# Walking two chunk loops in step: matmuls of RWKV and gated delta issued in pairs

## The chip, the core and the metric

The kernel runs on one core of a Trainium2 chip. A core has TensorE (PE in the profile; its weight loads are shown apart as PEld), VectorE (DVE), ScalarE (ACT), GpSimd (POOL) and SyncE (SP), which issues most DMAs. The engines run side by side, each through its own queue in order, and wait for one another by semaphores. SBUF is the working memory; matmuls write to PSUM, which has eight banks. The metric is the device time of one execution in microseconds (us).

## The reference

One layer of a hybrid encoder over 512 tokens of width 2048:

```python
y = xn @ w_in[l]
o_gdn = _gdn_group(...)      # gated delta: 8 heads of 128
o_rwkv = _rwkv_group(...)    # RWKV-7: 16 heads of 64
h = h + jnp.concatenate([o_gdn, o_rwkv], axis=-1) @ w_out[l]
h = h + _cross_attention(...)             # 4 heads, 256 memory tokens
h = h + jnp.square(jax.nn.relu(hn @ mlp_w_up[l])) @ mlp_w_down[l]
return _rmsnorm(h, norm_final)
```

Both groups carry a state along the sequence. Gated delta is written in the reference over chunks: with products that are known ahead (`W`, `U`, `Aqk`, the decayed keys), a step of its scan is

```python
v_new = U_c - W_c @ S
o = qd @ S + A_c @ v_new
S = S * exp(gl) + kt.T @ v_new
```

RWKV is written token by token (`S = S * w_t + (S a_t) b_t^T + v_t k_t^T`, `o = S r_t`), and the kernel computes it in chunks as well. Everything is in float32; the large products are done in the kernel as three products of parts in fp32r (high times high, low times high, high times low), the small ones in f32.

## The kernel before

The kernel has a mixer part (input projections, gated delta, RWKV, the key side of the attention's projections), then the rest of the attention with the output projection, then the MLP. The change is in the mixer.

**The filler.** `projections` computes the 59 columns of the input projection, called py in the profile: a column is 128 outputs by 512 tokens, 48 matmuls of 128x128 weights by 512 tokens in fp32r. `evict` multiplies a finished column by the norm's factor on DVE and puts it in one of four buffers (`NY = 4`, tile y), from which the mixer reads it. Two PSUM banks (mm) take turns, so the matmuls of a column wait for the eviction of the column two before. After the columns come the key projections kp (also in `projections`), and then kq, which waits for the event that the last inverse of gated delta is done (`after("inverted", 7)`). py, kp and kq need weights that `loader` splits into a high and a low part on ACT and DVE.

**The two chains.** The mixer goes in eight rounds. Round j takes seven columns: three for `rwkv(j)` (r, k, v of two heads, 128 channels) and four for `gdn(j)` (k, q, v, z of one head). Each function is a chain of operations on all engines:

- `rwkv(j)`: decay and keys (`pW`, `pA`, `pn`, then the event front); the Gram products of the 8 chunks for both heads (tiles pgA and pgB, in two halves of four chunks; 64 rows deep, 128 columns), masked into GA and GB by DVE; the 16x16 blocks' inverse on POOL by way of DRAM (`inverse_blocks`); transposes and products with 64x64 matmuls (pk, pat, pv, pak, pkv); the inverse's upper levels (ri); `pu` and `pwt`; the chunk loop over 8 chunks (tile rs); and the outputs (po, pp). `rwkv(j+1)` begins before the chunk loop of j, but its Gram products wait until po of j is done.
- `gdn(h)`: convolutions of the columns, norms (gn), products (pkk, pqk), transposes (pkt, pvt), its own blocks' inverse on POOL and the upper levels (gi), the chunk loop over 4 chunks (tile gs), the outputs (gpo, gon). `gdn(h+1)` begins when `gdn(h)` has ended.

A step of RWKV's chunk loop has two matmuls, WTz by the state and BTz by U, of 128 rows and 64 columns (14 in all); one of gated delta has three, of 128 rows and 128 columns (10 in all). Between two matmuls of a loop stands one DVE operation, which reads the PSUM result and makes the next operand. RWKV's loop uses the one bank scr, gated delta's the one bank scg. The POOL inverse of the two chains shares a lock (`solving`): the second may begin, its load of the blocks included, only when the first is through.

**The order of the work.** All of it is issued by a planner that runs while the kernel is built. Each chain is a generator that yields one operation, a list of operations to be issued together, or a condition. `run` keeps a model clock for each engine, asks each chain for its next operation, and takes the one whose modelled start is first:

```python
key = (t + (0 if c[3][0][0] == "PE" else 150 * rank), rank)
```

The rank decides between equal PE starts, and for other engines it adds 150 ns a step: evictions have rank 0, the loader 2, rwkv and gdn 3, the projections 4. So a matmul of a chain goes before a py matmul that could start at the same time, and py takes all the rest. `cost` prices an operation and `start` gives its earliest time from the modelled ends of its inputs. The prices move the model's clocks and with them the order in which the operations of each engine are issued; the chip then runs each engine's queue in this order.

`cost` charges an fp32r matmul 0.417 ns a column and 13.3 ns after another of its kind, 120 ns after any f32 matmul; an f32 matmul is charged 100 ns more where the shape of its weights differs from that before and is not 128x128.

Of the kernel before, what the change touches and what calls it, by code (L numbers as in the profile page):

```python
# [10 lines left out]
F32R = mybir.dt.float32r  # L11
# [62 lines left out]
def build(tc, I, out):  # L74
# [132 lines left out]
    SL, SM = Lane(nc.sync, "SP", wait=6000.0), Lane(nc.sync, "SP", margin=8000.0)  # L207
    DV, AC, GS, TE, SY = (Lane(e, k) for e, k in ((V, "DVE"), (S, "ACT"), (GP, "POOL"), (PE, "PE"), (nc.sync, "SP")))

    def cost(op):  # L210
        eng, nm, _, a, k, out, ins, _ = op
        n = out.free_size()
        if eng == "PE":
            l = ins[0]
            if l.dtype == F32R:
                return n * 0.417 + (13.3 if state["shape"] is None else 120.0)
            sh = (l.partition_size(), l.free_size())
            sw = 0 if state["shape"] == sh or sh == (128, 128) else 100
            if nm == "transpose":
                return sw + (110 if sh[0] > 64 else 40)  # L220
            if sh == (64, 64):
                return sw + (32 if op[5].tensor.name[:2] in ("ri", "gi", "pa", "pv", "pu", "pw", "pk", "po", "pp") else 59)
            if sh[0] < 128 and n == 512:
                return sw + 530
            return sw + (115 if sh[0] < 128 and n == 128 else 2 * max(n * 0.84, 114))
        if eng == "DVE":
            if nm == "memset":
                return 60 + 0.3 * n
            if nm == "tensor_scalar":
                return 210 + 0.45 * n  # L230
# [21 lines left out]
    def issue(op):  # L252
        eng, nm, f, a, k, out, ins, slack = op
        t = start(op)
        d = cost(op)
        f(*a, **k)  # L256
        if nm == "dma_start":
            clock[eng] = t + (60 if eng == "ACT" else 620 if any(x.tensor.name[:2] in ("bg", "nd") for x in [out] + ins) else 330)
            size = math.prod(out.shape) * 4
            state["dma"] = max(state["dma"], t + 330) + size / 300  # L260
            t, eng = max(state["dma"] + 700, t + 2900) + slack[1], "DMA"
        else:
            t += d
            clock[eng] = t
        if eng == "PE":
            state["shape"] = None if ins[0].dtype == F32R else (ins[0].partition_size(), ins[0].free_size())
        if eng == "ACT" and len(a) > 2 and a[2] in (AF.Tanh, AF.Ln, AF.Exp):
            state["table"] = "l" if a[2] == AF.Ln else "e"
        landed[where(out)] = (t, eng)
        for i in ins:  # L270
            b = where(i)
            if seen.get(b, (0.0, 0))[0] < t:
                seen[b] = (t, eng)
# [7 lines left out]
    def after(*ev):  # L281
        return lambda: ev in events
# [282 lines left out]
    def projections():  # L565
# [4 lines left out]
        for n in range(2, NIN):  # L570
            if n == NSQ[3] + 3:
                yield after("macc")
                pt = psb("pms", "mm", 2)
                mc = ybuf[macc[0]]
                yield TE.matmul(pt[:, 0:M], ones, mc[:, 0:M], start=True, stop=False)
                yield TE.matmul(pt[:, 0:M], ones, mc[:, M:2 * M], start=False, stop=True)
                chain(memnorm(pt, mc[:, M:2 * M]), 1)
            if n >= 4:
                yield after("py", n - 2)
            pt = psb(f"py{n}", "mm", 2)  # L580
            yield from gemm_([pt], xhi, xlo, 2 * n, left="x" if n == NIN - 1 else None)
            chain(evict(n, pt), 0)
# [264 lines left out]
        yield DV.tensor_copy(big[hA, :, 64:128], v(A[:, 256:512])[hA])  # L847


    def rwkv(j):  # L850
        base = 3 + 7 * j
        js = slice(j * P, (j + 1) * P)
# [54 lines left out]
        G = [tl(f"G{nm}", shape=[P, 8, P]) for nm in "AB"]  # L907
        GA, GB = G
        for q in range(2):
            pgs = [psb(f"pg{nm}{j}_{q}") for nm in "AB"]  # L910
            for c in range(4):
                for pg, h in zip(pgs[::-1], (hB, hA)):
                    yield TE.matmul(pg[:, c * P:(c + 1) * P], flat(BK[h, q * 4 + c]), flat(AR[h, q * 4 + c]),
                                    start=True, stop=True)
            for pg, g in zip(pgs, G):
                yield DV.tensor_tensor(out=g[:, q * 4:q * 4 + 4, :], in0=pg.rearrange("p (c t) -> p c t", t=P),
                                       in1=K("mA").unsqueeze(1).broadcast_to([P, 4, P]), op=ALU.mult)
# [102 lines left out]
        if j < 7:  # L1020
# [6 lines left out]
        yield DV.tensor_tensor(out=lgs[64:96, P:2 * P], in0=lg[64:96, P:2 * P], in1=lgs[64:96, P:2 * P].bitcast(F32),  # L1027
                               op=ALU.subtract)

        for c in range(7):  # L1030
            if c > 0:
                p1 = psb(f"rs1_{j}_{c}", "scr", 1)
                yield TE.matmul(p1[:, 0:64], WTz[:, c - 1, :], Qs[:, CS[c]], start=True, stop=True)
                yield DV.tensor_tensor(out=U[:, CS[c]], in0=p1[:, 0:64], in1=U[:, CS[c]], op=ALU.add)
            p3 = psb(f"rs3_{j}_{c}", "scr", 1)
            lm, nx = lam[:, c:c + 1], CS[c + 1]
            if c > 0:
                yield DV.scalar_tensor_tensor(out=Qs[:, nx], in0=Qs[:, CS[c]], scalar=lm, in1=Qs[:, nx],
                                              op0=ALU.mult, op1=ALU.add)
            yield TE.matmul(p3[:, 0:64], BTz[:, c, :], U[:, CS[c]], start=True, stop=True)  # L1040
            yield DV.scalar_tensor_tensor(out=Qs[:, nx], in0=p3[:, 0:64], scalar=lm, in1=Qs[:, nx],
                                          op0=ALU.mult, op1=ALU.add)
        p1 = psb(f"rs1_{j}_7", "scr", 1)
        yield TE.matmul(p1[:, 0:64], WTz[:, 6, :], Qs[:, CS[7]], start=True, stop=True)
        yield DV.tensor_tensor(out=U[:, CS[7]], in0=p1[:, 0:64], in1=U[:, CS[7]], op=ALU.add)
        if j < 7:
            yield after("front", j + 1)
# [29 lines left out]
    def gdn(h):  # L1077
# [99 lines left out]
        yield from inverse_levels(f"gi{h}", Tm, Tt, N3, ("gkn", "gk", "gqn"), TtG)  # L1177
        events.add(("inverted", h))
        vns, Ss = tl("gE"), tl("gEG")
        for c in range(4):  # L1180
            cs = slice(c * P, (c + 1) * P)
            r1 = vb[:, cs]
            if c > 0:
                p1 = psb(f"gs1_{h}_{c}", "scg", 1)
                yield TE.matmul(p1[:, 0:P], wd[:, cs], Ss[:, cs], start=True, stop=True)
                r1 = short(P, "sg")
                yield DV.tensor_tensor(out=r1, in0=vb[:, cs], in1=p1[:, 0:P], op=ALU.subtract)
            p2 = psb(f"gs2_{h}_{c}", "scg", 1)
            yield TE.matmul(p2[:, 0:P], TtG[:, c, :], r1, start=True, stop=True)
            yield DV.tensor_copy(vns[:, cs], p2[:, 0:P])  # L1190
            if c == 3:
                break
            p3 = psb(f"gs3_{h}_{c}", "scg", 1)
            yield TE.matmul(p3[:, 0:P], kt[:, cs], vns[:, cs], start=True, stop=True)
            nx = slice((c + 1) * P, (c + 2) * P)
            if c == 0:
                yield DV.tensor_copy(Ss[:, nx], p3[:, 0:P])
# [1201 lines left out]
```

## Time and profile before

| | us |
|---|---|
| three runs | 2908.32, 2912.63, 2914.87 |
| their median | 2912.63 |
| the profiled execution | 2911.43 |
| its span, first to last instruction | 2909.6 |
| mixer, from the span's start to the first kq | 1034.8 |
| PE busy | 2874.6 |
| DVE busy | 2331.9 |

The mean granted clock of TensorE is 0.997 of full speed. The prediction quotes lines of several views. A line of the timeline has the start in us, the duration in us, the engine, the line of the kernel (L256 is the planner's helper, which stands for all operations of the mixer), the operation, the tiles (written <- read), the shape, and how many records it merges. An f32 matmul leaves two records, an fp32r matmul one. The ends of matmuls are modelled and overlap with the next, so distances are taken from start to start. A row of the view by stretches has the stretch, its length, and the busy time of PE, PEld, DVE, ACT and POOL with the number of instructions, then the granted clock, the DMA share and GB/s; where it is asked for one tile, only the engines that touch the tile are listed. A row of the waits has who waited, for what, the total, the number of times and the longest. A row of a tile has the minimum, median and maximum duration in ns and the first and last start.

### The profile page before, as it was taken

Reading aid. Unit: us, or ns where it says so; the run is one execution under the profiler, and the core shown is the slowest. Engines: PE = TensorE matmul, PEld = TensorE weight load, DVE = VectorE, ACT = ScalarE, POOL = GpSimd, SP = SyncE. Lnnn points to the kernel's source line nnn. Section 1 sums busy time; section 2 is a strip of 40 time slices with the busy share of each in tenths; the row PEclk is TensorE's granted clock in tenths of the full one; section 3 lists DMA queues with packets and bytes.
Section 4 is the critical chain, followed back from the end, with each engine's and each line's share of the span. In section 5 each row is a group of like instructions: output and inputs, shape, how many; then the busy total and the mean of one; then the engine's idle time right before and its main releaser. Section 6 shows DMA issues by size and latency. Waiting matters only on the chain.

```text
span 2909.6 us, 49187 instructions
## 1 busy us (share of the span) xinstructions
PE 2874.6 (99%) x18794; PEld 2420.8 (83%) x18794; DVE 2331.9 (80%) x3547; ACT 1573.0 (54%) x2233; POOL 225.8 (8%) x547
## 2 busy tenths in 40 slices
PE   8999999999999999999999999999999999999998
PEld 7877777777777888889988888888888888888786
DVE  7787787787887877769946898899998878776998
ACT  6454555545656565664445556555555644454544
POOL 0213214223123000000000000000000000000000
PEclk9999999999999999999999999999999999999999
DMA  5647656656566688784323354566556878876633
GB/s 190 176 139 182 161 158 169 167 152 188 176 163 192 187 269 274 229 288 153 120 95 94 109 160 162 187 196 193 187 197 192 288 232 280 280 242 209 199 104 103
DMA packets 314300, 541.47 MB, mean 186 GB/s; under 512 B 100360, under 2 KB 185612, under 8 KB 314064
## 3 DMA queue, kind: packets, MB, share of 16 engines
q1 hardware_dynamic: 287824, 508.97, 56.8%
q10 hardware_dynamic: 26240, 29.37, 2.9%
q8 instruction: 147, 2.41, 0.3%
q14 instruction: 89, 0.73, 0.1%
HBM read 436.11 MB, written 102.12 MB: 185 GB/s over the span
## 4 chain that ended last, share of the span: by engine, by line
PE 94%; DMA 2%; DVE 2%; ACT 1%; issue 1%; POOL 0%; SPq 0%; ACTq 0%; DVEq 0%; POOLq 0%
PE py L256 21%; PE mxu L256 12%; PE mgu L256 6%; PE mgd L256 6%; PE mxd L256 6%; PE op L122 5%; PE vp L122 3%; PE kq L256 3%; PE kp L256 3%; PE sc L122 3%; PE at L122 3%; PE scgd L256 3%; PE scrd L256 3%; PE mmu L256 3%; PE mmd L256 3%; PE vo L122 2%
## 5 line engine op out<-in xcount | busy, mean ns | idle before, releaser
L256 ACT CAST whi<-wraw 128x1024 fp32r<-128x1024 f32 (+1 forms) x364 | 381.6, 1049 | 423.4 <-PE py L256 143.7
L256 DVE TENSOR_TENSOR wlo<-wraw,whi 128x1024 fp32r<-128x1024 f32 (+1 forms) x364 | 448.0, 1231 | 116.6 <-ACT whi L256 108.9
L256 PE MATMUL py<-xhi,whi 128*128 128x512 f32 x928 | 372.2, 401 | 8.0 <-ACT xhi L256 8.0
L256 PE MATMUL py<-xlo,whi 128*128 128x512 f32 x928 | 373.6, 403 | 0.0
L256 PE MATMUL py<-xhi,wlo 128*128 128x512 f32 x928 | 373.1, 402 | 0.0
L256 ACT CAST whi<-w 128x1024 fp32r<-128x1024 f32 x181 | 190.5, 1054 | 221.7 <-PE mxu L256 46.6
L256 DVE TENSOR_TENSOR wlo<-w,whi 128x1024 fp32r<-128x1024 f32 x181 | 220.8, 1222 | 54.1 <-ACT whi L256 53.5
L256 PE MATMUL mxu<-cb,whi 128*128 128x512 f32 x1016 | 255.0, 392 | 0.0
L256 PEld LDWEIGHTS py<-xhi,whi 128*128 128x128 f32 x928 | 175.2, 189 | 42.1 <-ACT xhi L256 8.0
L256 PEld LDWEIGHTS mxu<-cb,whi 128*128 128x128 f32 x1016 | 182.8, 189 | 32.7
L256 PEld LDWEIGHTS py<-xhi,wlo 128*128 128x128 f32 x928 | 175.1, 189 | 35.2 <-issue 1.8
L256 PEld LDWEIGHTS py<-xlo,whi 128*128 128x128 f32 x928 | 175.0, 189 | 35.1 <-DVE xlo L256 0.5
L131 DVE TENSOR_TENSOR wlo<-wraw,whi 128x1024 fp32r<-128x1024 f32 x112 | 136.8, 1223 | 45.4 <-ACT whi L130 44.2
L130 ACT CAST whi<-wraw 128x1024 fp32r<-128x1024 f32 x112 | 117.6, 1051 | 84.4 <-PE op L122 28.4
L256 PEld LDWEIGHTS mxu<-cb,wlo 128*128 128x128 f32 x1016 | 138.7, 190 | 10.5 <-DVE wlo L256 0.7
L256 PE MATMUL mxu<-cb,wlo 128*128 128x256 f32 x1016 | 142.2, 282 | 0.3 <-DVE wlo L256 0.3
L256 ACT ACT_TABLE_LOAD x87 | 111.6, 1283 | 35.9 <-DVE suml_gn L256 15.0
L256 PE MATMUL mgu<-cb,whi 128*128 128x512 f32 x512 | 129.4, 394 | 1.2 <-ACT whi L256 1.1
L256 PE MATMUL mxd<-whi,cb 128*128 128x512 f32 x512 | 127.8, 392 | 2.7 <-ACT whi L256 2.7
L256 PE MATMUL mgd<-whi,cb 128*128 128x512 f32 x512 | 126.6, 389 | 0.0
L256 PEld LDWEIGHTS mxd<-whi,cb 128*128 128x128 f32 x512 | 96.2, 188 | 23.8 <-ACT whi L256 3.5
L122 PE MATMUL op<-ob,whi 128*128 128x256 f32 (+1 forms) x752 | 115.3, 304 | 0.0
(944 smaller groups left out, 6637.6 us busy)
## 6 DMA issues: line engine op xcount, KB each, us to landing
wraw<-in_w_in SPq DMA_DIRECT2D x116, 512.0 KB, 4.5
wraw<-in_w_up SPq DMA_DIRECT2D x65, 512.0 KB, 3.7
w<-in_w_up SPq DMA_DIRECT2D x63, 512.0 KB, 3.8
ds<-in_w_dm SPq DMA_DIRECT2D x128, 205.0 KB, 4.1
sd_s<-ds SPq DMA_DIRECT2D x128, 205.0 KB, 5.2
w<-sd_s SPq DMA_DIRECT2D x48, 512.0 KB, 4.9
wraw<-sd_s SPq DMA_DIRECT2D x48, 512.0 KB, 4.8
wraw<-in_w_dm SPq DMA_DIRECT2D x46, 512.0 KB, 5.0
```

The costliest lines, as they stand in the source:

```text
L122: PE.matmul(o, l, r, start=start, stop=stop, skip_group_check=again)
L130: S.copy(hi, src)
L131: V.tensor_tensor(out=lo, in0=src, in1=hi.bitcast(F32), op=ALU.subtract)
L256: f(*a, **k)
```

## The change

- **Pairs.** A helper `meet(key, ops)`: the chain that comes first leaves its operations under a key and waits for an event; the chain that comes second yields both lists as one, which the planner issues together, and sets the event. In the rounds below 5, the last ten of the 14 matmuls of RWKV's loop and the ten of gated delta's loop meet one by one. The first four of RWKV go alone. In the last three rounds nothing meets.
- **Gram products.** The second half of pgA and pgB takes the two banks mg (used by gated delta) in place of the banks mx that the first half uses. The order of the generator is as before: eight matmul calls, the two maskings on DVE, the next eight calls, their maskings.
- **Prices.** `cost` tells three kinds of PE work: fp32r (0), f32 with 128 rows (1), f32 with fewer rows (2). Going into kind 2 costs 92 ns; leaving it costs 223 (to fp32r) or 116 (to kind 1); fp32r after kind 1 costs 88.
- **A wait.** Before the memory norm's chain is started, `projections` waits until the column before has been evicted.

```diff
+    def shape_of(l):
+        return None if l.dtype == F32R else (l.partition_size(), l.free_size())
+
+    def kind(sh):
+        return 0 if sh is None else 1 if sh[0] == 128 else 2
 ...
+            was, now = kind(state["shape"]), kind(shape_of(l))
+            sw = (0, 0, 92)[now] if was != 2 else (223, 116, 0)[now]
             if l.dtype == F32R:
-                return n * 0.417 + (13.3 if state["shape"] is None else 120.0)
+                return n * 0.417 + 13.3 + (88 if was == 1 else sw)
             sh = (l.partition_size(), l.free_size())
-            sw = 0 if state["shape"] == sh or sh == (128, 128) else 100
 ...
+                yield after("py", n - 1)
                 chain(memnorm(pt, mc[:, M:2 * M]), 1)
 ...
+    waiting = {}
+
+    def meet(key, ops):
+
+        if key in waiting:
+            yield waiting.pop(key) + ops
+            events.add(key)
+        else:
+            waiting[key] = ops
+            yield after(*key)
 ...
-            pgs = [psb(f"pg{nm}{j}_{q}") for nm in "AB"]
+            pgs = [psb(f"pg{nm}{j}_{q}", ("mx", "mg")[q]) for nm in "AB"]
 ...
+        step = iter(range(-4, 99))
+        joint = lambda op: meet(("m", j, k), [op]) if 0 <= (k := next(step)) < 10 and j < 5 else [op]
 ...
-                yield TE.matmul(p1[:, 0:64], WTz[:, c - 1, :], Qs[:, CS[c]], start=True, stop=True)
+                yield from joint(TE.matmul(p1[:, 0:64], WTz[:, c - 1, :], Qs[:, CS[c]], start=True, stop=True))
 ...
-            yield TE.matmul(p3[:, 0:64], BTz[:, c, :], U[:, CS[c]], start=True, stop=True)
+            yield from joint(TE.matmul(p3[:, 0:64], BTz[:, c, :], U[:, CS[c]], start=True, stop=True))
 ...
-            yield TE.matmul(p2[:, 0:P], TtG[:, c, :], r1, start=True, stop=True)
+            yield from meet(("m", h, next(step)), [TE.matmul(p2[:, 0:P], TtG[:, c, :], r1, start=True, stop=True)]) if h < 5 else [TE.matmul(p2[:, 0:P], TtG[:, c, :], r1, start=True, stop=True)]
```

The two other matmuls of gated delta's loop and the last one of RWKV's are wrapped in the same way.

More of the change, by code (lines that the diff above doesn't have):

```diff
@@ L265, in issue @@
         if eng == "PE":
-            state["shape"] = None if ins[0].dtype == F32R else (ins[0].partition_size(), ins[0].free_size())
+            state["shape"] = shape_of(ins[0])
         if eng == "ACT" and len(a) > 2 and a[2] in (AF.Tanh, AF.Ln, AF.Exp):
@@ L1043, in rwkv @@
         p1 = psb(f"rs1_{j}_7", "scr", 1)
-        yield TE.matmul(p1[:, 0:64], WTz[:, 6, :], Qs[:, CS[7]], start=True, stop=True)
+        yield from joint(TE.matmul(p1[:, 0:64], WTz[:, 6, :], Qs[:, CS[7]], start=True, stop=True))
         yield DV.tensor_tensor(out=U[:, CS[7]], in0=p1[:, 0:64], in1=U[:, CS[7]], op=ALU.add)
@@ L1179, in gdn @@
         vns, Ss = tl("gE"), tl("gEG")
+        step = iter(range(10))
         for c in range(4):
@@ L1184, in gdn @@
                 p1 = psb(f"gs1_{h}_{c}", "scg", 1)
-                yield TE.matmul(p1[:, 0:P], wd[:, cs], Ss[:, cs], start=True, stop=True)
+                yield from meet(("m", h, next(step)), [TE.matmul(p1[:, 0:P], wd[:, cs], Ss[:, cs], start=True, stop=True)]) if h < 5 else [TE.matmul(p1[:, 0:P], wd[:, cs], Ss[:, cs], start=True, stop=True)]
                 r1 = short(P, "sg")
@@ L1193, in gdn @@
             p3 = psb(f"gs3_{h}_{c}", "scg", 1)
-            yield TE.matmul(p3[:, 0:P], kt[:, cs], vns[:, cs], start=True, stop=True)
+            yield from meet(("m", h, next(step)), [TE.matmul(p3[:, 0:P], kt[:, cs], vns[:, cs], start=True, stop=True)]) if h < 5 else [TE.matmul(p3[:, 0:P], kt[:, cs], vns[:, cs], start=True, stop=True)]
             nx = slice((c + 1) * P, (c + 2) * P)
```

## The prediction

> **What bounds the kernel now.** First the page: its span, its busy times and the chain that ended last.
>
> ```profile
> span 2909.6 us, 49187 instructions
> PE 2874.6 (99%) x18794; PEld 2420.8 (83%) x18794; DVE 2331.9 (80%) x3547; ACT 1573.0 (54%) x2233; POOL 225.8 (8%) x547
> PE 94%; DMA 2%; DVE 2%; ACT 1%; issue 1%; POOL 0%; SPq 0%; ACTq 0%; DVEq 0%; POOLq 0%
> ```
>
> TensorE (PE) is busy 99% of the span and is 94% of the chain. The change touches only the mixer, which ends where kq begins, at 1035 us (row below). The view by stretches, one row for a middle round, one for the handover from the input projections (py) to the key projections (kp):
>
> ```profile
> 547.00:659.00 112.00, 111.24 (x1030) 88.77 (x1030) 87.12 (x163) 59.51 (x83) 29.32 (x67) 1.00 0.59 163
> ...
> 884.00:935.00 51.00, 46.46 (x504) 37.29 (x502) 34.78 (x62) 28.37 (x48) 13.87 (x38) 0.97 0.75 208
> ```
>
> A round of about 112 us leaves PE 0.8 us idle; only the handover loses more, 4.5 us. Among PE's waits from 104 to 1035 us stand
>
> ```profile
> PE gn L256 <- DVE suml_gn L256: 2.2, 4, 0.7
> ...
> PE rs L256 <- DVE Qs L256: 0.7, 1, 0.7
> ```
>
> So the two chunk loops wait for nothing that PE does not fill with py matmuls. Time is won only by taking work from PE, and lost when a delay of the chains leaves PE without py or kp to fill in. The filler's price is in the chain: 30 py in 6.81 us, 0.227 us each.
>
> ```profile
> 351.38 6.81 PE py L256 x30
> ```
>
> **The pairs.** In rounds 0 to 4, ten rs matmuls of RWKV (64 columns) are issued each next to a gs matmul of gated delta (128 columns): 50 pairs. Each f32 matmul leaves two records. The timeline shows an rs alone, a gs alone, and an rs inside a burst of eight pqk records:
>
> ```profile
> 499.36 0.39 PE L256 MATMUL py<-xhi,wlo 128*128 128x512 f32 x1
> 499.59 0.33 PE L256 MATMUL rs<-BK,BTz 128*128 128x64 f32 x2
> ...
> 500.04 0.39 PE L256 MATMUL py<-xlo,whi 128*128 128x512 f32 x1
> ```
>
> ```profile
> 526.48 0.40 PE L256 MATMUL py<-xhi,wlo 128*128 128x512 f32 x1
> 526.71 0.39 PE L256 MATMUL gs<-gEG,gq 128*128 128x128 f32 x2
> ...
> 527.17 0.39 PE L256 MATMUL py<-xlo,whi 128*128 128x512 f32 x1
> ```
>
> ```profile
> 265.38 0.39 PE L256 MATMUL py<-xlo,whi 128*128 128x512 f32 x1
> ...
> 266.27 0.33 PE L256 MATMUL rs<-Qs,WTz 128*128 128x64 f32 x2
> ...
> 266.95 0.39 PE L256 MATMUL py<-xhi,whi 128*128 128x512 f32 x1
> ```
>
> Between the py before and the second py after lie two py (0.455 us) and the excursion. rs alone: 500.04 - 499.36 - 0.455 = 0.225 us. gs alone: 0.69 - 0.455 = 0.235. The burst of ten records: 1.57 - 0.455 = 1.115, or 0.1115 a record. A pair has four records: 0.446 in a burst against 0.225 + 0.235 = 0.460 apart. That saves 0.014, and I take 0.006 because the rows round to 0.01: 50 x 0.006 = **-0.3 us**. The upper bound takes the 64-column rs at half the price of a 128-column record pair (0.112) and all the rest as a switch that the pair saves: 50 x 0.118 = -5.9 us. I stay at the low end because rs costs the same 0.22 inside the burst, where nothing switches. On the loss side a pair is held until both operands are there. PE takes its matmuls in order, so py stands behind a late pair and with it the eviction of its column; on DVE the two answers of a pair stand in one queue, and the splits of py's weights behind them. The row of rs waits shows 0.7 us in one wait; three such make +2, my bound.
>
> [...]
>
> **The Gram products.** Each round has two halves of 16 records, 64 rows deep. Their second half takes the banks mg in place of mx, so it no longer waits for DVE to empty the first. The view by stretches for pgB alone, and the timeline of an unbroken half (round 0) and a broken one (round 4):
>
> ```profile
> 93.00:100.00 7.00, 2.31 (x16) 1.93 (x16) 1.21 (x2) 1.00 0.28 79
> ...
> 541.00:549.00 8.00, 2.57 (x16) 2.00 (x16) 1.36 (x2) 1.00 0.83 254
> ...
> sum 58.00, PE 20.06 PEld 15.85 DVE 7.82; mean PE 2.51 PEld 1.98 DVE 0.98
> ```
>
> ```profile
> 93.49 0.39 PE L256 MATMUL py<-xlo,whi 128*128 128x512 f32 x1
> ...
> 95.24 0.39 PE L256 MATMUL py<-xhi,whi 128*128 128x512 f32 x1
> ```
>
> ```profile
> 544.98 0.39 PE L256 MATMUL py<-xhi,wlo 128*128 128x512 f32 x1
> ...
> 546.16 0.50 PE L256 MATMUL gon<-suml_gon,onesr 128*128 128x512 f32 x1
> 546.50 0.40 PE L256 MATMUL gon<-sumh_gon,onesr 128*128 128x512 f32 x1
> ...
> 547.81 0.40 PE L256 MATMUL py<-xlo,whi 128*128 128x512 f32 x1
> ```
>
> Unbroken: 95.24 - 93.49 - 0.455 = 1.295 us. Broken in two by gon: 2.83 less four full matmuls (0.91) = 1.92. A break costs 0.63. pgB's busy time is 2.31 in an unbroken round and 0.26 more per break, so the sum has (20.06 - 8 x 2.31) / 0.26 = 6 breaks. RWKV moves away from gon (below); I take five of six as gone: **-3.2 us**. Will the halves join into one burst? In the kernel's order the two DVE copies of the first half stand between them. The planner puts such an operation at its start plus 450 ns, and py goes ahead meanwhile, so a gap of some six py remains. If they did join, at most one more break's price per round would go, 8 x 0.63 = 5.0. Bounds 0 to -3.8 - 5.0 = -8.8.
>
> **Where RWKV moves.** The parts of round 4, each with its first and last start:
>
> ```profile
> L256 PE MATMUL rs<-Qs,WTz x14: 217/274/323, 605.8 to 624.2; 128*128 128x64 f32 x14
> ...
> L256 PE MATMUL gs<-gv,TtG x2: 272/274/275, 634.1 to 634.2; 128*128 128x128 f32 x2
> ...
> L256 PE MATMUL gs<-sg,TtG x6: 270/272/274, 640.9 to 651.6; 128*128 128x128 f32 x6
> ...
> L256 PE MATMUL po<-AR,Qs x12: 218/218/267, 634.9 to 635.2; 64*64 64x64 f32 x12
> ...
> L256 PE MATMUL pgB<-AR,BK x16: 272/272/373, 654.5 to 659.4; 64*128 64x128 f32 x16
> ```
>
> RWKV's loop is over before gated delta's begins. Walking in step, its first four matmuls go alone, and then it stands until 634.1; it ends near 652, po comes at 653 instead of 634.9, and the next round's pgB at 672. All of RWKV is 18 us later in rounds 1 to 5. The last three rounds win it back: po there stands some 10 us behind the loop's end (624.2 to 634.9), waiting for the next round's front.
>
> That delay I cost at nothing. Its cover is the column buffers (four). Five evictions and the readers of three columns, and the eviction of v5:
>
> ```profile
> L256 DVE TENSOR_TENSOR y<-py,rstd x5: 692/692/692, 592.5 to 661.5; 128x512 f32<-128x512 f32 x5
> ...
> L256 DVE SCALAR_TENSOR_TENSOR gz<-sg,y x1: 682/682/682, 615.5 to 615.5; 128x512 f32<-128x512 f32 x1
> ...
> L256 DVE SCALAR_TENSOR_TENSOR k<-y,dp,k x1: 744/744/744, 623.5 to 623.5; 128x512 f32<-128x512 f32 x1
> ...
> L256 DVE SCALAR_TENSOR_TENSOR r<-y,dp,r x1: 745/745/745, 640.1 to 640.1; 128x512 f32<-128x512 f32 x1
> ```
>
> ```profile
> 626.51 0.69 DVE L256 TENSOR_TENSOR y<-py,rstd 128x512 f32<-128x512 f32 x1 [0.86 <-PE py L256]
> ```
>
> 18 us later k is read at 641 and r at 658; at 626.5 only r and k hold buffers, so the eviction still finds one. But if gated delta slips too, its gz stands in the way of that eviction from 11 us on, and the column before it somewhat later; I take 15 us as the cover. Beyond it evictions wait, and py with them: each us of delay is then a us of idle PE. On POOL, gated delta's inverse queues behind RWKV's, which is now 18 us later:
>
> ```profile
> 571.57 1.29 POOL L256 TENSOR_TENSOR gEs<-gE,cst 128x512 f32<-128x512 f32 x1
> ...
> 596.53 0.21 POOL L256 TENSOR_TENSOR sgj<-sgi 32x15 f32<-32x15 f32 x1 [23.25 <-DMA sgi<-ndgi]
> ```
>
> RWKV's block there ends at 571.6 and would end at 590. The lock between the two lets gated delta's load go out on SP only then, just in time for 596.5; a round with a shorter gap is pushed. At the end of the mixer kq waits for the last inverse:
>
> ```profile
> 1034.84 0.39 PE L256 MATMUL kq<-khl,whi 128*128 128x512 f32 x1
> ```
>
> ```profile
> L256 PE MATMUL gi7u<-TtG,gkn x8: 218/218/267, 1005.7 to 1006.1; 64*64 64x64 f32 x8
> ```
>
> It is done 29 us before kq's start at 1035, so some lag at the end is free as well.
>
> **Other edits, together.** The planner's prices only move its clocks; no instruction is added. They move DVE's and ACT's order, bounded by the waits quoted, 2.9 us either way; I take 0. The wait for py's eviction before the memory norm issues nothing: the next py column takes the bank of that eviction anyway; 0.
>
> **Sum.** The profiled run took 2911.43 us (span 2909.6 and 1.8 around it), 1.2 below the median 2912.63. -0.3 - 3.2 = -3.5 gives 2907.9, rounded 2908; from the median it would be 2909.1.
>
> **Rivals.**
> (1) Slower: the joint loop holds gated delta. Its chain never waits for a column (r5, the first of the five evictions, at 592.5, is read at 640.1; the others too lie ready), so a longer loop lengthens every round. A step of rs takes 1.4 us (605.8 to 624.2 in 13), one of gs 1.75 (634.1 to 651.6 in ten). Overlapped, ten joint steps take 17.5 us as now; one after the other 31; half-way 24. Five rounds of 6.5 more are 32 us of lag, less a cover of 15: +17, 2928. It decides from 3 us a round on, 15 in five. For it: both answers sit in a DVE that is busy 87.12 of 112 us. Against: RWKV is there 10 us early, so only the step's own pace counts. 0.26.
> (2) The pairs save their upper bound, and the Gram breaks all go: -5.9 - 3.8 = -9.7: 2901.7; with the halves joined as well 2896.7. Against: the burst row. 0.24.
> (3) The change doesn't do what it says: the breaks come back at other places, the pairs save nothing: 2911, give or take 2. 0.16.
>
> **How the numbers follow.** The forecast has 0.34, with 2902 to 2911 as its own range. 0.2% of the median is 5.8 us, about what a measurement of this kernel can tell from no change; that line is at 2906.8. Faster: (2) and somewhat under half of the forecast, 0.24 + 0.15 = 0.39. Same: the rest of the forecast and (3), 0.19 + 0.16 = 0.35. Slower: (1), 0.26. The range runs from (2) with the halves joined, 2897, to (1), 2928.
>
> **What would show it.** The Gram step is right if pgB's busy time stands at 2.31 in nearly every round and py still lies between the halves. The pair step is right if rs and gs alternate in rounds 0 to 4 and the four records of a pair cost 0.45 us beyond py; rival (2) is right if they cost 0.34. The move is right if pgB of rounds 1 to 5 comes some 18 us later against gs, and POOL's inverse of gated delta starts no later than before. The prediction is wrong by (1) if a gs loop takes over 20 us, evictions come late, and PE is busy less than 111 of 112 us in a round.

## The result, and the profile after

The kernel is slower: 2918.69 us (median of 18 runs) against 2910.69 for the kernel before (18 runs beside it). The ratio is 1.0026, 95% interval 1.0019 to 1.0033, or some 8 us. The prediction was 2908, between 2897 and 2928: the time lies in the range, on the side to which 0.26 was given. The profiled execution took 2915.88 us, 4.5 more than that of before.

The page of the kernel after, its span, busy times and chain:

```profile
span 2914.1 us, 49200 instructions
PE 2870.8 (99%) x18794; PEld 2420.6 (83%) x18794; DVE 2339.0 (80%) x3547; ACT 1565.8 (54%) x2227; POOL 227.6 (8%) x547
PE 96%; DVE 2%; DMA 1%; ACT 1%; issue 0%; SPq 0%; ACTq 0%; DVEq 0%
```

PE is still nearly the whole chain. Its own work fell by 3.8 us, from 2874.6 to 2870.8. That is close to the 3.5 us that the prediction had summed up. But the span grew by 4.5, so PE idles about 8 us more. The view by stretches says where:

```profile
547.00:659.00 112.00, 110.81 (x976) 88.37 (x972) 83.67 (x154) 53.35 (x75) 24.93 (x65) 1.00 0.62 172
884.00:935.00 51.00, 40.65 (x346) 32.38 (x346) 32.00 (x56) 27.47 (x47) 15.23 (x34) 0.93 0.71 198
```

The middle round is still full (110.81 of 112; 111.24 before). In the handover from py to kp PE worked 40.65 of 51 us, 46.46 before: 5.8 us lost there. PE's waits from 104 to 1135 us name it:

```profile
PE kp L263 <- ACT whi L263: 7.8, 1, 7.8
PE gn L263 <- DVE suml_gn L263: 1.8, 2, 1.1
```

One kp, at 922.7 us, waits 7.8 us in one piece for whi, the split of its weights on ACT. Before, the same wait was 1.2:

```profile
PE kp L256 <- ACT whi L256: 1.2, 1, 1.2
```

The two steps of the change itself, first the Gram products (view by stretches, pgB alone, round 4 and the sum over the eight rounds):

```profile
545.00:553.00 8.00, 2.31 (x16) 1.93 (x16) 0.68 (x1) 1.00 0.38 119
...
sum 61.00, PE 18.75 PEld 15.49 DVE 7.21; mean PE 2.34 PEld 1.94 DVE 0.90
```

and a pair in the timeline of round 4:

```profile
644.50 0.39 PE L263 MATMUL py<-xlo,whi 128*128 128x512 f32 x1
644.73 0.33 PE L263 MATMUL rs<-BK,BTz 128*128 128x64 f32 x2
644.90 0.44 PE L263 MATMUL gs<-gv,TtG 128*128 128x128 f32 x2
645.09 0.48 PE L263 MATMUL py<-xhi,wlo 128*128 128x512 f32 x1
645.41 0.40 PE L263 MATMUL py<-xhi,whi 128*128 128x512 f32 x1
```

pgB's sum is 18.75 = 8 x 2.31 + 0.27: one break is left of six. The pair costs 645.41 - 644.50 - 0.455 = 0.455 us; the median of the 48 pairs that stand between py matmuls is 0.45, against 0.446 predicted. And RWKV's place against gated delta's loop, round 4 (groups of one tile; the two last numbers are the first and last start):

```profile
L263 PE MATMUL gs<-gv,TtG x2: 275/302/328, 644.9 to 645.1; 128*128 128x128 f32 x2
...
L263 PE MATMUL gs<-sg,TtG x6: 275/302/328, 650.1 to 658.3; 128*128 128x128 f32 x6
...
L263 PE MATMUL po<-AR,Qs x12: 218/218/267, 659.0 to 659.3; 64*64 64x64 f32 x12
```

In this round the joint loop takes 13.4 us, against 17.5 for gated delta's alone before. Over rounds 0 to 4 the difference is small: the mean loop took 14.1 us after and 14.6 before, where it ran from 10.7 us in round 0 to 17.5 in rounds 3 and 4. RWKV's output po now follows the loop's end by 0.7 us; before it stood 16.7 us ahead of it (634.9 against 651.6).

### The profile page after: what moved, and what is told of

It reads as the page before. It is cut to its first block, busy times and chain, and to the rows that moved or that the text cites. A ratio compares the mean times of both kernels' runs of the same rounds, so it can differ in the third digit from the quotient of the medians.

```text
span 2914.1 us, 49200 instructions
## 1 busy us (share of the span) xinstructions
PE 2870.8 (99%) x18794; PEld 2420.6 (83%) x18794; DVE 2339.0 (80%) x3547; ACT 1565.8 (54%) x2227; POOL 227.6 (8%) x547
## 3 DMA queue, kind: packets, MB, share of 16 engines
q1 hardware_dynamic: 287824, 508.97, 56.2%
## 4 chain that ended last, share of the span: by engine, by line
PE 96%; DVE 2%; DMA 1%; ACT 1%; issue 0%; SPq 0%; ACTq 0%; DVEq 0%
PE py L263 22%; PE mxu L263 12%; PE mgu L263 6%; PE mgd L263 6%; PE mxd L263 6%; PE op L122 5%; PE vp L122 3%; PE kq L263 3%; PE mmu L263 3%; PE sc L122 3%; PE at L122 3%; PE scgd L263 3%; PE vo L122 3%; PE scrd L263 3%; PE kp L263 3%; PE mmd L263 3%
## 5 line engine op out<-in xcount | busy, mean ns | idle before, releaser
L263 PEld LDWEIGHTS mgd<-whi,cb 128*128 128x128 f32 x512 | 96.1, 188 | 20.0
```

## Experiments

Theories at the outset. T1: the pairs end both loops at one time, the tails of the two chains compete for DVE and ACT, gated delta's cycle grows, and its lag is paid at the handover. T1b: the handover's stall is a local accident of SP's queue. T2: prices or banks did it, not the pairs. T3, T4 and T5 came later and are given where they are first used. All kernels compute the whole.

This table has every run that follows. Where it says "pairs" with a number, that many rounds are paired (ten pairs in each). "Cycle" is the mean distance between the starts of gated delta's loops in rounds 0 to 4; "gaps" is the sum of all stretches over 0.45 us without a matmul, from the first matmul to the first vp (the value projections, behind kq). Both are taken from the profiled execution.

| kernel | ratio to before | 95% | cycle us | gaps us |
|---|---|---|---|---|
| before | 1 | | 111.4 | 6.9 |
| after (5 pairs) | 1.0026 | 1.0019-1.0033 | 117.9 | 14.8 |
| e1 after, no pairs | 0.9999 | 0.9990-1.0007 | 115.2 | 8.1 |
| e2 pairs alone | 1.0165 | 1.0151-1.0179 | 120.1 | 36.1 |
| e4 Gram bank alone | 1.0035 | 1.0023-1.0047 | 114.2 | 15.5 |
| e5 prices alone | 1.0019 | 1.0010-1.0028 | 114.7 | 8.9 |
| e7 after, 3 pairs | 0.9992 | 0.9983-1.0001 | 114.1 | 8.8 |
| e6 after, 8 pairs | 1.0092 | 1.0078-1.0106 | 118.2 | 27.7 |
| e8 before, price +1 ns | 1.0038 | 1.0026-1.0051 | 114.9 | 15.9 |
| e16 before, price -1 ns | 1.0107 | 1.0093-1.0121 | 111.8 | 30.6 |
| e9 after, price +1 ns | 1.0067 | 1.0054-1.0079 | 119.3 | 22.6 |
| e10 after, price -1 ns | 1.0131 | 1.0118-1.0144 | 120.2 | 30.9 |
| e11 no pairs, price +1 ns | 1.0003 | 0.9995-1.0012 | 113.5 | 9.4 |
| e12 no pairs, price -1 ns | 1.0018 | 1.0010-1.0027 | 115.4 | 10.8 |
| e3 gE's load on ACT | 1.0016 | 1.0006-1.0027 | 117.8 | 12.7 |
| e13 RWKV's tail waits | 1.0160 | 1.0146-1.0174 | 122.0 | 38.6 |
| e14 e13, price +1 ns | 1.0152 | 1.0138-1.0166 | 121.5 | 37.0 |
| e15 e13, price -1 ns | 1.0171 | 1.0157-1.0185 | 124.4 | 45.6 |
| e17 gEs on VectorE | 1.0078 | 1.0065-1.0091 | 117.9 | 26.2 |
| e18 e13 and e17 | 1.0114 | 1.0096-1.0131 | 121.6 | 28.7 |

### The parts one by one: e1, e2, e4, e5

e1, no pairs: in all four places of the two loops

```diff
-j < 5 else [op]
+j < 0 else [op]
-if h < 5 else [TE
+if h < 0 else [TE
```

> The changed kernel with no paired rounds; the Gram products in one burst and the new prices stay. Theory T1 (the pairs end both loops at one time, the two tails then compete for VectorE and ScalarE, gated delta falls behind by some 4 to 8 us in each paired round, and the handover to kp pays for it): the lag goes, gon follows the end of the gs loop by 6 to 7 us in every round again (7.6 to 13 in the changed kernel), the load of gE for the last head is issued near 891 us and not at 914, the wait of kp on whi falls from 7.8 us to under 1.5, the stretch 884:935 holds about 46.5 us of PE and not 40.7, and the time is that of before less the 3 us of the Gram products: 2905 to 2911. Rival T2 (prices or banks reorder the work and make the lag, the pairs do not): 2916 to 2920, with the wait of kp still there.

e2, the pairs alone: one bank for the Gram products and the prices of before.

```diff
-            pgs = [psb(f"pg{nm}{j}_{q}", ("mx", "mg")[q]) for nm in "AB"]
+            pgs = [psb(f"pg{nm}{j}_{q}") for nm in "AB"]
-            sw = (0, 0, 92)[now] if was != 2 else (223, 116, 0)[now]
+            sw = 0 if state["shape"] == sh or sh == (128, 128) else 100
```

> The pairs alone: the Gram products keep the one bank and the prices of the kernel before. T1: the lag and the wait of kp on whi stay, the Gram products cost their 3 us again, 2918 to 2923. T2 (prices or banks make the loss): 2908 to 2913, no wait of kp on whi above 2 us.

e4: the kernel before with only the second bank (the first line of that diff the other way round).

> The kernel before with the Gram products' two halves in two banks, neither pairs nor new prices. T1: nothing of the lag; the six breaks become one or two in each round, worth 2 to 3.5 us: 2907 to 2909. T2 with the bank as the cause (the second bank takes the place of another tile's and holds it up): 2912 or more.

e5: the kernel before with only the new prices.

> The kernel before with the new prices alone: one bank for the Gram products, no pairs. T1 (a paired round's chain of gated delta takes 114 to 122 us where a round's work of TensorE takes 111, so each paired round adds some 6 us of lag; the prices only move the start of the first round, pkk from 130.0 to 119.5 us): the first pkk near 119.5, periods of the gs loop of 112 to 114 on average, no gain and no loss at the end: 2908 to 2914. T3 (any edit reorders the whole stage, and the order alone decides over some +/- 8 us; the Gram bank alone cost 9): anything between 2904 and 2922, with gaps of TensorE at other places.

Measured: e1 2911.75 beside 2912.09, e2 2959.53, e4 2921.35 (before in these three 2912.09), e5 2917.56 beside 2911.22. In e1 the handover is that of before again; its row and its wait:

```profile
884.00:935.00 51.00, 46.50 (x555) 37.42 (x554) 34.09 (x60) 28.03 (x49) 15.35 (x34) 0.93 0.73 209
```

```profile
PE kp L263 <- ACT whi L263: 4.0, 1, 4.0
```

46.50 and gE's load at 888.7 us were foretold, a wait under 1.5 was not (4.0), nor that gon would follow the loop by 6 to 7 us everywhere (5.7 to 9.5). Without the pairs the loss is gone, so T2 falls as the whole story. But the cycle is still 115.2 us: more than half of its growth from 111.4 to 117.9 stands here too, with the earlier start of the first loop (174.2 us, 188.5 before), and no loss follows from it. The 3 us of the Gram products do not show in e1's time: vp starts 1.6 us earlier (1123.3, before 1124.9), and the part behind it, which the change does not touch, took 2 us longer in that execution, which nothing here explains. But e2 is a surprise of the same sign, six times as large: the pairs alone cost 47 us, and kp's wait for whi, which T1 had stay, is only 1.1 us there. Instead the filler runs dry. PE's waits, and the place of one of them in the timeline:

```profile
PE py L256 <- DVE y L256: 13.2, 4, 4.2
```

```profile
522.12 0.80 PE L256 MATMUL py<-xhi,whi 128*128 128x512 f32 x1 [3.81 <-DVE y L256]
522.71 0.63 PE L256 MATMUL py<-xlo,whi 128*128 128x512 f32 x1
523.14 0.63 PE L256 MATMUL py<-xhi,wlo 128*128 128x512 f32 x1
```

py waits for the eviction of a column (y), which stands on DVE behind chain work (three operations on gv take 2.32 us from 519.02 us on, and the eviction starts at 521.37). That is the case in the prediction's words "beyond it evictions wait, and py with them". And e4 and e5, edits that save or move next to nothing, cost 9 and 6 us. So a third theory is needed, T3: each edit reorders the whole stage, and the order alone is worth several us.

### How much an order is worth: e8, e16, e9 to e12

The same edit in three kernels (before, after, after without pairs), up and down:

```diff
-                return n * 0.417 + 13.3 + (88 if was == 1 else sw)
+                return n * 0.417 + 14.3 + (88 if was == 1 else sw)
```

> The kernel before with one price of the planner raised by 1 ns of some 227 (the constant of a full matmul from 13.3 to 14.3), nothing else; a measure of what another order of the same work is worth. T1 holds the order for nearly neutral: 2908 to 2914. T3: the order alone moves the time by 3 us or more from 2911, either way, and the gaps of TensorE stand at other places.

> The kernel before with the constant of a full matmul lowered from 13.3 to 12.3. Raised by 1 ns it took 2922.7, unchanged 2911. If the order of before is a good one among its neighbours: 2914 to 2924. If the raised one was the odd case: 2908 to 2914.

> The changed kernel with one price of the planner raised by 1 ns (the constant of a full matmul 13.3 to 14.3). The same nudge moved the kernel before by 11 us, so one order proves little; five pairs and no pairs are compared here over three orders each (with the two already run, 2918.7 and 2911.8). T1 (the pairs lengthen gated delta's cycle): this order too lies above its partner without pairs, by 4 to 12 us: 2916 to 2926. T3 (the order alone decides): anywhere in 2906 to 2926, the mean of the three with pairs within 3 us of the mean of the three without.

> The changed kernel with the same price lowered by 1 ns (13.3 to 12.3). T1: 2916 to 2926, 4 to 12 us above its partner without pairs. T3: anywhere in 2906 to 2926.

> The changed kernel without pairs and with that price raised by 1 ns. T1: 2908 to 2916, the gs loop of round 6 starts near 857 us and vp near 1123 (in all kernels run so far but the one with eight pairs vp starts 260 to 267 us after that loop). T3: anywhere in 2906 to 2926.

> The changed kernel without pairs and with that price lowered by 1 ns. T1: 2908 to 2916. T3: anywhere in 2906 to 2926.

Measured: the kernel before took 2922.68 with the price up and 2941.19 with it down. One ns in a price that the chip never sees moves it by 11 and 31 us, the second further than either case expected: its own order is the best of the three. In the one 31 us slower, one wait carries much of it:

```profile
PE kp L256 <- DVE y L256: 12.9, 1, 12.9
PE gn L256 <- DVE suml_gn L256: 6.2, 3, 4.5
```

So T3 is right as far as a single order proves little, and no single difference of 10 us here can be put down to its edit. Nor do the gaps carry all of it: in e5 they are 2 us over those of before and the time 6. Over three orders each, though, five pairs took 2918.7, 2931.2 and 2950.5, and no pairs 2911.8, 2912.3 and 2916.7. The two nudged orders with pairs lie above what T1 and T3 expected, and T3's own test, means within 3 us, is far from met. The best with pairs is behind the worst without, though the intervals of these two overlap. In ratios to the kernel before beside them the means are 1.0075 and 1.0007, which makes the pairs about 20 us dear (0.0068 x 2912; 8, 19 and 33 in the single orders). The place of the loss is not the same in them: before 860 us lie 3.9 of the 14.8 us of gaps in the change's own order, but 14.0 of 22.6 and 23.8 of 30.9 in the nudged two, spread over the rounds in e9 and mostly between 740 and 860 us in e10. Banks and prices together are the other way round: against the kernel before at the same price they are at -0.0001, -0.0035 and -0.0089. (The wait ahead of the memory norm is in all kernels made from the changed one; it was not run alone.) The whole change costs 0.0026, 0.0029 and 0.0024 in the three.

### The dose: e7 and e6

The numbers 5 of the diff above become 3, or 8.

> The changed kernel with three paired rounds instead of five. T1: two paired rounds less, some 10 us less of lag, so the load of gE for the last head is issued near 900 us and not at 914, the handover idles 4 to 6 us and not 11, and the time is between that of no pairs (2911.8) and of five (2918.7): 2910 to 2915. T3: no trend, 2906 to 2924.

> The changed kernel with all eight rounds paired instead of five. T1: the periods of the gs loop stay near 118 us in rounds 5 to 7 too (111 on average in the changed kernel for rounds 5 and 6), the last gs loop starts 15 to 20 us later than at 1030, and as the cover is used up the time goes to 2928 to 2945. T3: no trend with the number of paired rounds, 2910 to 2924.

Measured: 2909.51 (beside 2911.22) and 2939.59. With 0, 3, 5 and 8 paired rounds: 0.9999, 0.9992, 1.0026, 1.0092. Three cost nothing in this one order, and whether they gain anything is open (the interval ends at 1.0001). With eight, rounds 5 and 6 took 114 and 113 us, not the 118 foretold, and the last loop started at 1041 and not 1030, 11 us later where 15 to 20 were foretold; PE's waits grew in the last rounds (pkk 5.1, gn 8.8 us). The trend is what T1 and not T3 foretold; but each dose was run in one order, and the orders of one kernel lie up to 31 us apart, so the trend alone does not prove it.

### The handover: e3

```diff
-        yield SL.dma_start(E, Rd[h:h + 1, :].broadcast_to([P, T]))
-        yield SL.dma_start(B, Rd[32 + h:33 + h, :].broadcast_to([P, T]))
+        LE = Lane(nc.scalar, "ACT") if h == 7 else SL
+        yield LE.dma_start(E, Rd[h:h + 1, :].broadcast_to([P, T]))
+        yield LE.dma_start(B, Rd[32 + h:33 + h, :].broadcast_to([P, T]))
```

> The changed kernel with the last head's two loads (gE and its partner) issued on ScalarE's queue, so that they do not stand behind the load of bg16T on SP, which waits for GpSimd. If the handover's stall is made by that queue (T1 at its last link, and T1b, which holds the queue alone guilty): gE lands near 913 us and not at 920, whi follows near 916, kp's wait falls from 7.8 us to 1 or 2, the time falls by 5 to 7 us, to 2911 to 2914; the lag of gated delta (its last loop near 1025 us) stays. If the lag itself is the cost and the queue only where it shows, another wait takes the place: 2916 to 2919.

The kernel after, ACT's timeline and the loads on SP ahead of it:

```profile
920.25 0.63 ACT L263 ACTIVATE gEG<-gE 128x512 f32<-128x512 f32 x1 [5.62 <-DMA gE<-Rd]
...
921.61 1.04 ACT L263 CAST whi<-wraw 128x1024 fp32r<-128x1024 f32 x1
```

```profile
904.57 0.33 SPq L263 DMA_DIRECT2D wraw<-in_memT  x1
911.26 0.58 SPq L263 DMA_DIRECT2D bg16T<-sr  x1
...
914.30 0.40 SPq L263 DMA_DIRECT2D gE<-Rd  x1
914.80 0.54 SPq L263 DMA_DIRECT2D wraw<-in_wk  x1
```

SP stands from 905 to 911 us at bg16T, which waits for RWKV's inverse on POOL (its last step ends at 911.2); behind it stand gE and kp's weights; on ACT the exponential of gE stands ahead of the split. In e3 gE's load was issued at 907.5 us (914.3 in the kernel after); with the 5.8 us from issue to landing that are the median of these loads in that kernel, gE was there at 913.3 by estimate, as foretold, and kp still waited 6.5 us:

```profile
914.67 0.58 SPq L263 DMA_DIRECT2D bg16T<-sr  x1
...
917.26 0.39 SPq L263 DMA_DIRECT2D wraw<-in_wk  x1
```

```profile
923.49 1.04 ACT L263 CAST whi<-wraw 128x1024 fp32r<-128x1024 f32 x1 [5.36 <-DMA wraw<-in_wk]
```

The load of the weights itself is caught behind bg16T. The time, 2915.68 (1.0016), is 3 us better by the ratios, less than the 5 to 7 hoped for and within what an order is worth. T1b holds in this sense: in this order SP's queue is where the lag turns into idle time, and gE was only one of two things in it. That the weights would have come in time without bg16T ahead of them was not tried.

### What makes the cycle longer: e13, e14, e15

In the paired rounds gated delta's norm gon comes up to 13 us after the loop (546.2 against a loop's end of 539.2 before; 548.8 against 535.8 after). T1 puts that down to RWKV's tail. T4: the meeting itself ties RWKV to gated delta, RWKV's lead is gone, and a later tail makes it worse. RWKV's tail is put back until that norm is issued:

```diff
         if j < 7:
             yield after("front", j + 1)
+        if j < 5:
+            yield after("gnorm", j)
...
         yield from rsq_(sq, pn, 1.0 / 128, b_eps6)
+        events.add(("gnorm", h))
```

> The changed kernel, five pairs, but in paired rounds RWKV's tail (po and after) is taken up only when gated delta's norm after the loop has been issued. Tail collision (T1): gon follows the loop by 6 to 8 us again and not by 12.8, the load of gE by 20 to 22 us and not by 24 to 29, the periods of the gs loop fall to 111 to 115, and the time goes to 2908 to 2916. Rival T4 (the meeting itself is the cost: RWKV, some 25 us early before, now has no slack, and its tail 8 us later makes it the late one): gon is early again, but the time stays at 2918 or rises, up to 2935.

> The same with the price raised by 1 ns; its partner without the wait measured 2931.2. T1: 2910 to 2920. T4: 2926 or more.

> The same with the price lowered by 1 ns; its partner without the wait measured 2950.5. T1: 2912 to 2925. T4: 2940 or more.

Measured: 2957.52, 2953.99, 2959.90 (before 2909.76 beside them). gon came 5.4 to 6.7 us after the loop, so the collision was taken away, and the cycle rose from 118-120 to 121.5-124.4. The first two runs were slower than their partners without the wait by 39 and 23 us, the third by 9; e13 lies even above T4's range. So T1's collision is not needed for a long cycle, and T4's later RWKV costs, in all three orders. Whether the collision adds anything of its own stays open, since the edit took it away and put RWKV back by 10 us at once. One round in three kernels shows the way it goes (tile groups and POOL's timeline, from the end of gated delta's loop 2 to the end of its loop 3). Of before's five rounds this is the one with the longest lead: po comes 15.5 to 24.7 us ahead of the loop's end in them, and the next loop ends 109.7 to 115.7 us after it; in the kernel after, po comes 0.7 us behind the loop's end each time, and the next loop ends 113.5 to 122.5 us after it. Before:

```profile
L256 PE MATMUL gs<-sg,TtG x6: 270/273/377, 421.3 to 429.5; 128*128 128x128 f32 x6
L256 PE MATMUL po<-AR,Qs x12: 218/218/218, 404.7 to 405.0; 64*64 64x64 f32 x12
444.52 0.21 POOL L256 TENSOR_TENSOR sr<-sr 64x15 f32<-64x15 f32 x1 [21.27 <-DVE wlo L256]
L256 PE MATMUL pkk<-gk,gkn x8: 273/275/275, 469.4 to 470.1; 128*128 128x128 f32 x8
484.55 0.52 POOL L256 TENSOR_TENSOR sgj<-sgi 32x15 f32<-32x15 f32 x1 [22.78 <-DMA sgi<-ndgi]
L256 PE MATMUL gs<-sg,TtG x6: 270/273/275, 528.6 to 539.2; 128*128 128x128 f32 x6
```

After:

```profile
L263 PE MATMUL gs<-sg,TtG x6: 275/302/328, 411.1 to 420.6; 128*128 128x128 f32 x6
L263 PE MATMUL po<-AR,Qs x12: 218/218/267, 421.3 to 421.6; 64*64 64x64 f32 x12
447.90 0.66 POOL L263 TENSOR_TENSOR sr<-sr 64x15 f32<-64x15 f32 x1 [21.24 <-ACT Kt L263]
L263 PE MATMUL pkk<-gk,gkn x8: 273/275/275, 467.4 to 468.2; 128*128 128x128 f32 x8
481.65 0.27 POOL L263 TENSOR_TENSOR sgj<-sgi 32x15 f32<-32x15 f32 x1 [16.62 <-DMA sgi<-ndgi]
L263 PE MATMUL gs<-sg,TtG x6: 275/302/328, 527.6 to 535.8; 128*128 128x128 f32 x6
```

e13, with RWKV's tail put back:

```profile
L263 PE MATMUL gs<-sg,TtG x6: 275/302/328, 422.6 to 431.8; 128*128 128x128 f32 x6
L263 PE MATMUL po<-AR,Qs x12: 218/218/267, 442.1 to 442.4; 64*64 64x64 f32 x12
469.99 1.04 POOL L263 TENSOR_TENSOR sr<-sr 64x15 f32<-64x15 f32 x1 [21.54 <-DMA sr<-ndri]
L263 PE MATMUL pkk<-gk,gkn x8: 272/275/275, 488.0 to 488.8; 128*128 128x128 f32 x8
500.15 0.20 POOL L263 TENSOR_TENSOR sgj<-sgi 32x15 f32<-32x15 f32 x1 [14.82 <-DMA sgi<-ndgi]
L263 PE MATMUL gs<-sg,TtG x6: 275/302/328, 545.1 to 554.3; 128*128 128x128 f32 x6
```

From the loop's end, in the order before, after, e13: po at -24.8, +0.7, +10.3; RWKV's inverse on POOL (sr) begins at +15.0, +27.3, +38.2; pkk at +39.9, +46.8, +56.2; gated delta's inverse (sgj) at +55.1, +61.0, +68.3; the next loop ends at +109.7, +115.2, +122.5. RWKV's next Gram products wait until po is done, its inverse follows from them, and gated delta's inverse comes behind it. Unpaired, RWKV runs ahead and there is slack in this ring; paired, po comes last, and the slack is used up: 25.5 us of po's delay cost 12.3 at RWKV's inverse and 5.5 at the loop's end; the next 9.6 cost 10.9 and 7.3.

The three kernels without pairs (e1, e11, e12) bear this out, and show that pairing is not the only way to lose the lead. In eight of their 15 rounds po is 9 to 24 us ahead of the loop's end, and the next loop ends 101 to 117 us after it; in the other seven po is only 5 to 6 us ahead, and it ends after 112 to 128. There a late round is followed by an early one sooner or later. With pairs every round is a late one. (This is seen side by side, not tested.)

RWKV's place is not all. At the same price the mean joint loop of rounds 0 to 4 took 14.1, 13.7 and 14.5 us with pairs and 12.9, 11.9 and 11.8 without, 1.3 to 2.6 us more, where the cycles are 2.7, 5.9 and 4.8 us longer. So some two fifths of what the pairs add to the cycle is the pace of the joint loop itself.

### Which queue hands it over: e17, e18

T5: gEs, gated delta's own operation on POOL, stands behind RWKV's inverse, and pkk behind gEs.

```diff
-        yield GS.tensor_tensor(out=c3(Es), in0=c3(E), in1=K("sneg")
+        yield DV.tensor_tensor(out=c3(Es), in0=c3(E), in1=K("sneg")
```

e17 is the kernel after with this, e18 is e13 with this.

> The changed kernel, five pairs, with gEs computed on VectorE and not behind RWKV's inversion on GpSimd. T5 (GpSimd's queue hands RWKV's delay to gated delta): in the rounds in which pkk followed gEs at once (pkk 46.8 us after the loop's end, gEs 42 to 44) pkk comes 2 to 5 us earlier; in the others (pkk 50 to 52), where gated delta's own tail is late, nothing; the period falls from 117 to about 114, 2910 to 2917. RWKV's own cycle as the cause: no change beyond that of an order, 2914 to 2932, pkk where it was.

> The run with RWKV's tail put back (2957.5), with gEs on VectorE. T5: pkk comes 40 to 47 us after the loop's end and not 55 to 56, gated delta's inversion starts right behind RWKV's on GpSimd, at 51 to 56 us and not at 67, the period falls from 122 to 111 to 116, and the time to 2912 to 2935. RWKV's own cycle as the cause: pkk comes earlier, but the period stays at 119 or more, because the joint loop then waits for RWKV, and the time stays above 2940.

Measured: 2934.03 and 2946.16 (before 2912.04). In e17 gEs ended 38.5 to 41 us after the loop and not at 41.5 to 44, and pkk did not move (46.8 to 51.4). In e18 pkk came at 51 to 52.5 and not 55 to 56, but gated delta's inverse stayed at 65.5 to 68.4. Both cycles stayed (117.9, 121.6). T5 falls. In e18 SP's timeline shows the next queue in line:

```profile
363.57 0.58 SPq L263 DMA_DIRECT2D bg16T<-sr  x1
...
368.87 2.62 SPq L263 DMA_DIRECT2D E<-bg16U  x4
...
372.23 1.25 SPq L263 DMA_DIRECT2D ndgi<-gEs  x2
...
376.43 0.33 SPq L263 DMA_DIRECT2D sgi<-ndgi  x1
```

The store and load of gated delta's blocks stand behind bg16T, which waits for RWKV's inverse, and its followers: they are issued 8.7 and 12.9 us after it. Whether that queue alone carries the delay was not tried and stays open. The other reason in e18's expectation is not seen either: the joint loop did not wait for RWKV, whose fourth rs came 19.8 to 23.6 us ahead of it in the paired rounds. Both execution times are above the ranges that T5 gave, e17's also above its rival's (2914 to 2932). So what is shown is that a later RWKV lengthens the cycle, and that the delay reaches gated delta between pkk and its inverse when it does not reach it at gEs. The opposite, RWKV put earlier in the paired rounds, was not run.

No kernel here is shown to beat the one before.

## Why the prediction was wrong, point by point

- **The pairs, -0.3: right in size.** 0.45 us a pair (median), 0.446 predicted. The upper bound of 5.9 is ruled out, and rival (2) with it.
- **The Gram products, -3.2: right.** One break left of six, the halves not joined. PE's work fell by 3.8 in all, 3.5 predicted; that these agree so closely is in part luck, since it fell by 1.8 in e1 and by 5.0 in e7, with the same bank in both. In e4 the same bank without the rest gained nothing; its order lost more than the bank saved.
- **Where RWKV moves: the place was right, the price wrong.** po's move against the loop's end was given as 18 us (634.9 to 653) and is 17.4. The next pgB moved less, from 2.9 us behind the loop's end (654.5) to 10.8, since before it did not start at once when po was done. "That delay I cost at nothing" is the step that failed. The cover in columns was weighed for evictions alone and for one round. The trace's path was written down, "gated delta's inverse queues behind RWKV's", with "a round with a shorter gap is pushed", but it was not summed over five rounds. The sign set for it failed: gated delta's inverse on POOL was to start no later than before, and in round 2 it starts 61.0 us behind the loop's end in place of 55.1 (rows above). Over three orders the cycle is 117.9 to 120.2 us with pairs and 113.5 to 115.4 without, and about 111 us of PE work a round (111.24 in the row of before) cannot fill it. After the paired rounds gated delta is late: the loop of round 6 began at 867.4 us, 856.8 without pairs (e1) and 858.7 before. Over three orders the pairs measured about +20 us, in place of the 0 for the delay.
- **The lag at the end is free: right, and at the wrong end.** The last inverse came 22 us later (1028.4, 1006.1 before) and kq only 2 (1036.8):

```profile
L263 PE MATMUL gi7u<-TtG,gkn x8: 218/218/267, 1027.9 to 1028.4; 64*64 64x64 f32 x8
```

  In this order the loss came at the handover, where SP, standing at RWKV's last inverse, held kp's weights; in the nudged orders most of it came before. No step priced either.
- **The prices, 0, plus or minus 2.9: the bound was far too narrow.** It came from waits that the trace of before shows, but a new order makes new waits: one price moved by 1 ns gave +11 and +31 us, the prices alone +6, the bank alone +9.
- **Rival (1): its sign and its lag, its mechanism in part.** Of its tests only the last was met, narrowly: PE was busy 110.81 of 112 us, less than 111; the joint loops took 13.4 to 15.6 us, not over 20, and py waited for an eviction only once, 0.5 us. But they are 1.3 to 2.6 us longer than loops without pairs at the same price, below the 3 us a round at which the rival was to decide. The rest of the longer cycle goes with po behind the loop's end. Its price of a gs step, 1.75 us, is too low for the round that it was read from (17.5 us are nine distances of ten matmuls, 1.94 each) and that round was one of the two slowest; in round 0 the loop took 10.7 us.
- **Rival (3)**, that the change does nothing, falls: all its savings are there.

## What to carry to other kernels

When two chains are made to meet, ask what each did with its lead: here RWKV's lead kept a ring open (output, next Gram products, inverse, the other chain's inverse), and a cycle longer than a round's PE work can be a loss however full PE looks in that round (117.9 to 120.2 us with pairs, about +20 us; e1's 115.2 brought none); it shows where the filler runs out, here at the handover and in other orders in the rounds before it. Where a planner sets the order, judge an edit over several orders (one price nudged either way), since a single one can be off by more than the edit is worth. A saving in PE's busy time says what the edit saves, and PE's gaps say what its order costs: read both.

## What the runs showed of the hardware

Behind three stalls PE's matmuls ran slower for a while, so that these stalls cost more than their length. After the gap of 3.81 us in e2 (rows above) the next py matmuls start 0.427 us apart (four starts from 522.71 to 523.99 us), where 0.227 is usual. After the 7.8 us at the handover of the kernel after, a kp pair (512 and 256 columns) takes 0.64 us and not 0.355 (from 924.6 to 926.5 us); the granted clock there is 0.50 in every stretch from 920.0 to 926.5 us and 1.00 from 927.0 us on, which gives the row of 884 to 935 us its 0.93 (0.97 before). The kernel before shows the same 0.64 us a kp pair (from 918.6 to 919.8 us) after an idle stretch of only 2.17 us and a burst of eight f32 records of pkk: its granted clock is still 1.00 in the idle stretch and up to 916.6 us, 0.50 from 917.0 to 920.1 us and then 1.00. What brings the lower clock, and after how short a gap, no run here settles. The change's own instructions took what the trace of before had let expect: a pair 0.45 us (median; 0.446 predicted), pgB 2.31 us in each of the seven rounds without a break (2.31 in the unbroken rounds of before).
